# Gate pieces spread over background steps, and high and low part of the activations in one product of 512 columns

## The chip, the core and the metric

The kernel runs on one core of a Trainium2 chip as one program. The metric is the device time of one execution in microseconds (us); three runs of the kernel before have a median of 1888.35 us (1887.22 to 1891.27). The engines are named as the profile names them: PE is TensorE's matmul and PEld its weight load, DVE is VectorE, ACT is ScalarE, POOL is GpSimd and SP is SyncE. An engine works off its own queue in the order written; a DMA is issued by an engine's queue ("ACTq" is an issue on ScalarE's queue).

## What is computed

One decoder block on 256 tokens of width 2048: a gated mixer, and then PEER, a layer that picks 128 of 16384 one-neuron experts per token (8 heads, 16 each). The change touches only PEER:

```python
q = (x @ w_query).reshape(T, 8, 2, 128)               # 16 column tiles of 128
s1, s2 = q[:, :, 0] @ sub_keys_1.T, q[:, :, 1] @ sub_keys_2.T
v1, i1 = top_k(s1, 16); v2, i2 = top_k(s2, 16)        # per half, then of the 16*16 sums
gates = softmax(top_k(v1[:, None] + v2[None, :], 16)) # 8*16 gates per token
act = gelu(x @ expert_down.T)                         # all 16384 experts: 128 tiles of 128
y   = (gates * act) @ expert_up                       # only rows that some token uses
```

The kernel computes the activation of every expert, and turns the gates into a dense array (expert by token), stored beside the activations in a scratch array in HBM, agD. From this it makes a list of the experts used, gathers their rows of agD and of expert_up, and multiplies.

## The kernel before

**Products in two parts.** A float32 matrix is split into a high part H (the value rounded to the format that TensorE takes at one column per cycle) and a low part L, the rest. Activations stand in hF, [128, 16, 2, 256]: for each of 16 slices k of the width, the high part of 256 tokens (index 0) and behind it the low part (index 1). A product is three products: H by high, H by low, L by high; `gemm_k` issues them for one k, 256 columns each, all into the same 256 columns of a PSUM bank:

```python
mm(o, H[:, ks], hT[:, k, 0, :], start=first, stop=False)     # L161
mm(o, H[:, ks], hT[:, k, 1, :], start=False, stop=False)     # L162
mm(o, L[:, ks], hT[:, k, 0, :], start=False, stop=last)      # L163
```

**The tiles.** A tile of weights is 128 by 2048, 1 MB, in one of three buffers raw, loaded by SP. `load_split` (L139) splits it in two halves of 1024: H by ACT (L152), L by DVE (L153). There are three buffers for H and three for L, so a half can be split when TensorE has ended the half three before it. 16 tiles make the queries (names ps_q; the first two are worked side by side), then 128 tiles the activations (ps_z). After a query tile ACT copies the sums to SBUF (`q_copy`, L588), and TensorE multiplies them by the keys (ps_sc, L595). After a down tile ACT applies gelu to the PSUM bank (L1034), and every fourth tile its queue issues the store of four of them to agD (L1036).

**The background.** Beside these products the rest of PEER runs as a list of pieces, bg, each with an estimated cost, in this order: top-k of the 8 heads for token tile 0, softmax, gates of chunk 0; top-k of four heads for tile 1, gates of chunk 1; the other four, softmax; a modulation vector (`adas`, 8 pieces, each a 1 MB load and two DVE passes), chunk 2, the second modulation vector, chunk 3; then the list of experts used (`list_a` to `list_d`). After each tile, `background(step)` takes pieces as long as their summed cost is below BG_RATE times the step. A chunk is 64 tokens: 8 gate units (one-hot products, ps_G, copied to the buffer gch), then 8 pieces `gate_out`, each a store of 16 experts per partition to agD on ACT's queue (L720, 512 KB in runs of 256 B) and a maximum over the chunk on DVE (L722, L725).

The framework sets the order on each engine: it takes the program's dependencies and priorities and writes one queue per engine; H and L have a raised priority. What stands in an engine's queue waits for what stands ahead of it.

**The end.** The last down tile's activations are not stored: they are multiplied by their gates (da, L1054), split (dWH, dWL, L1056 and L1058) and multiplied by the last rows of expert_up (24 products, ps_y, L1065), while the first blocks of the list are gathered (agr, uraw). Then follows a loop over the blocks of the list (L1179), which the change leaves alone.

Of the kernel before, what the change touches and what calls it, by code (L numbers as in the profile page):

```python
# [8 lines left out]
F32 = mybir.dt.float32  # L9
# [4 lines left out]
AF = mybir.ActivationFunctionType  # L14
ALU = mybir.AluOpType
# [25 lines left out]
HP2 = 200  # L41
# [3 lines left out]
def block_kernel(ctx: ExitStack, tc: tile.TileContext, I: dict, out: bass.AP):  # L45
    nc = tc.nc
# [11 lines left out]
    def bank(name):  # L58
        return psp.tile([P, 512], F32, tag="bank", name=name)
# [105 lines left out]
    def gemm_t(src, hT, name, order=tuple(range(KT))):  # L165
        HL = load_split(src)
        ps = bank(name)
        for n, k in enumerate(order):
            gemm_k(ps[:, :T], HL, hT, k, n, n == 0, n == KT - 1)
        return ps  # L170

    def rstd_bcast(ps, tmp_pool, name):
        sd = tmp_pool.tile([P, T], F32, tag="rstd", name=name + "_sd")
# [366 lines left out]
    k = 0  # L540
# [172 lines left out]
    def gate_out(ch, part):  # L713
        tt = ch * TCH // P
        w = P // GP
        sl = slice(part * w, (part + 1) * w)
        g = gch[ch][:, sl, :]
        cs = slice(T + ch * TCH, T + (ch + 1) * TCH)
        e_ = min(sl.stop, NS_E)
        nc.scalar.dma_start(agV[:, sl.start : e_, cs], gch[ch][:, sl.start : e_, :])  # L720
# [6 lines left out]
        if part == GP - 1:  # L727
            nc.scalar.activation(
                gl[:, ch * TCH : (ch + 1) * TCH], gch[ch][:, P - 1 : P, :].rearrange("p a t -> p (a t)"), AF.Copy
            )  # L730
            if ch * TCH % P:
                nc.vector.memset(mk[tt][:, P - 1 : P], 0.0)


# [6 lines left out]
    V = nc.vector  # L741

    def list_a():
        gp_cm[0].__exit__(None, None, None)
        m0, m1, mB, used = lt("la", 4)
        mA, mC, one, tri = lt("lb", 4)
        sA, sB, sC, w = lt("lc", 4)
# [163 lines left out]
    bg = []  # L911

    def topk1(tt, h):
        bg.append((2 * h + 2, 2.4, lambda: topk_a(tt, h)))
        bg.append((2 * h + 2, 4.0, lambda: topk_b(tt, h)))

    def gates(ch):
        n = TCH // 8
        for u in range(n * ch, n * ch + n):
            bg.append((0, 3.1, lambda u=u: gate_unit(u)))  # L920
        for part in range(GP):
            bg.append((0, 9.4 / GP, lambda part=part: gate_out(ch, part)))

    def adas(b):
        for _ in range(8):
            bg.append((0, 2.4, lambda: ada_f[b].piece()))

    def x1_all():
        x1_nat(0)
        x1_nat(1)  # L930
        xp_cm.__exit__(None, None, None)

    bg.append((1, 1.0, x1_all))
    for h in range(8):
        topk1(0, h)
    bg.append((0, 2.0, lambda: softmax(0)))
    gates(0)
    for h in range(4):
        topk1(1, h)
    gates(1)  # L940
    for h in range(4, 8):
        topk1(1, h)
    bg.append((0, 2.0, lambda: softmax(1)))
    adas(0)
    gates(2)
    adas(1)
    gates(3)
    bg.append((0, 8.0, list_a))
    bg.append((0, 5.0, list_b))
    for c in range(16):  # L950
        bg.append((0, 2.5, lambda c=c: list_c(c)))
    bg.append((0, 2.0, list_d))
    bgi = 0
    spent = 0.0

# [9 lines left out]
    for h in range(8):  # L965
        if h == 0:
            pq = [bank("ps_q0"), bank("ps_q1")]
            w2 = [load_raw(I["w_q"][i]) for i in range(2)]
            for half in range(2):
                parts = []  # L970
                for i in range(2):
                    H = wp.tile([P, 1024], F32R, tag="H", bufs=3, name="H")
                    L = wp.tile([P, 1024], F32R, tag="L", bufs=3, name="L")
                    r = w2[i][:, half * 1024 : (half + 1) * 1024]
                    nc.scalar.activation(H, r, AF.Copy)
                    nc.vector.tensor_tensor(L, r, H.bitcast(F32), op=ALU.subtract)
# [23 lines left out]
        )  # L1000

    def open_up():
        ex_cm.__exit__(None, None, None)
        up = R["up"] = ctx.enter_context(tc.tile_pool(name="up", bufs=1, reuse_waits="tile"))
        R["raw"] = [wp.tile([P, 2048], F32, tag="araw", bufs=2, name="uraw") for _ in range(2)]
        R["ag"] = [up.tile([P, 2 * T], F32, name=f"agr{i}") for i in range(NA)]
        R["H"] = [up.tile([P, 2048], F32R, name=f"uH{i}") for i in range(NS)]
        R["L"] = [up.tile([P, 2048], F32R, name=f"uL{i}") for i in range(NS)]
        R["WH"] = [up.tile([P, T], F32R, name=f"uWH{i}") for i in range(NW)]
        R["WL"] = [up.tile([P, T], F32R, name=f"uWL{i}") for i in range(NW)]  # L1010
        R["z"] = up.tile([P, P], BF16, name="zst")
        R["zm"] = up.tile([P, 512], BF16, name="zmv")
        nc.gpsimd.memset(R["z"], 0.0)
        nc.gpsimd.memset(R["zm"], 0.0)
        for b in range(2):
            gather(R["raw"][b], I["up"], idxU, b)
# [10 lines left out]
    actg = None  # L1027
    done_at = NE
    for j in range(NE):
        ps = gemm_t(I["down"][j], hF, "ps_z")  # L1030
        if j % AB == 0:
            actg = ag.tile([P, AB, T], F32, tag="actg", bufs=2, name="actg")
        if j < NE - 1:
            nc.scalar.activation(actg[:, j % AB, :], ps[:, :T], AF.Gelu)  # L1034
        if j % AB == AB - 1 and j < NE - 1:
            nc.scalar.dma_start(agV[:, j - AB + 1 : j + 1, 0:T], actg)  # L1036
        elif j == NE - 2:
            nc.scalar.dma_start(agV[:, j - j % AB : j + 1, 0:T], actg[:, : j % AB + 1, :])
# [10 lines left out]
    nc.scalar.activation(actg[:, (NE - 1) % AB, :], ps[:, :T], AF.Gelu)  # L1049


    dH, dL = load_split(I["up"][NE * P - P : NE * P, :])
    da = up.tile([P, T], F32, name="dact")
    nc.vector.tensor_tensor(da, actg[:, (NE - 1) % AB, :], gl, op=ALU.mult)  # L1054
    dWH = up.tile([P, T], F32R, name="dWH")
    nc.scalar.activation(dWH, da, AF.Copy)  # L1056
    dWL = up.tile([P, T], F32R, name="dWL")
    nc.vector.tensor_tensor(dWL, da, dWH.bitcast(F32), op=ALU.subtract)  # L1058
# [264 lines left out]
```

## Time and profile before

| | |
|---|---|
| median of three runs | 1888.35 us |
| the profiled execution | 1886.62 us, of which its span 1884.8 us |
| mixer, to the first query product | 0 to 509 us |
| queries and down tiles | 509 to 1445 us |
| last down tile's own products and start of the last loop | 1445 to 1461 us |
| loop over the list, end | 1461 to 1885 us |
| PE, DVE, ACT busy | 1796 (95%), 1435 (76%), 875 us (46%) |

The span is the time between the first and the last instruction; the rest of the execution, 1.8 us, lies around it. A busy share is an average over stages; the stage that the change touches is the second.

### The profile page before, as it was taken

How to read it: one execution, taken by the hardware profiler on the slowest of the kernel's cores; microseconds unless marked ns; L12 is line 12 of the kernel's file. 1: busy time of each engine (PE TensorE's matmuls, PEld its weight loads, DVE VectorE, ACT ScalarE, POOL GpSimd, SP SyncE). 2: the span in 40 equal slices, each digit the busy share in tenths (PEclk: the TensorE clock that was granted, in tenths of full speed). 3: DMA queues.
4: the chain of work that ended last, by engine and by line, in shares of the span. 5: the costliest groups of instructions: out<-in, count | busy, mean ns of one | idle time of the engine just before them, and what ended most of it. 6: DMA issues, size and time to landing. Idle time of an engine off the chain costs nothing. (4 is left out here: it accounts for less than half of the span.)

```text
span 1884.8 us, 31863 instructions
## 1 busy us (share of the span) xinstructions
PE 1796.2 (95%) x12820; PEld 1628.0 (86%) x12820; DVE 1434.8 (76%) x2248; ACT 875.1 (46%) x1157; POOL 257.9 (14%) x231
## 2 busy tenths in 40 slices
PE   5889999999999999999999999989998999999995
PEld 3336999999899999999999999989997788888884
DVE  6886889888779877977887777766653777777776
ACT  1116554544554554454345535533343555555654
POOL 0000000000000000000000000000001655656660
PEclk8999999999899999999999999989999999999998
DMA  9996888778565558748787695775565899989992
GB/s 380 352 359 264 342 317 315 272 270 323 189 225 178 190 174 248 225 171 238 230 297 263 196 358 198 218 216 179 179 242 175 321 393 337 324 310 339 320 336 90
DMA packets 153294, 497.21 MB, mean 264 GB/s; under 512 B 75976, under 2 KB 92232, under 8 KB 102064
## 3 DMA queue, kind: packets, MB, share of 16 engines
q1 hardware_dynamic: 47560, 327.55, 47.8%
q0 software_dynamic: 22400, 129.92, 19.0%
q10 hardware_dynamic: 83176, 37.56, 7.3%
q8 instruction: 109, 1.79, 0.4%
q14 instruction: 49, 0.40, 0.1%
HBM read 457.49 MB, written 37.50 MB: 263 GB/s over the span
## 5 line engine op out<-in xcount | busy, mean ns | idle before, releaser
L152 ACT ACTIVATE H<-raw 128x1024 fp32r<-128x1024 f32 x390 | 411.9, 1059 | 575.9 <-PE ps_z L162 386.5
L153 DVE TENSOR_TENSOR L<-raw,H 128x1024 fp32r<-128x1024 f32 x390 | 473.8, 1220 | 227.7 <-ACT H L152 226.0
L161 PE MATMUL ps_z<-hT_f,H 128*128 128x256 f32 x2048 | 586.3, 286 | 7.2 <-ACT H L152 7.2
L163 PE MATMUL ps_z<-hT_f,L 128*128 128x256 f32 x2048 | 581.4, 284 | 5.2 <-DVE L L153 5.2
L162 PE MATMUL ps_z<-hT_f,H 128*128 128x256 f32 x2048 | 581.3, 284 | 0.0
L161 PEld LDWEIGHTS ps_z<-hT_f,H 128*128 128x128 f32 x2048 | 394.5, 193 | 9.5 <-ACT H L152 7.7
L163 PEld LDWEIGHTS ps_z<-hT_f,L 128*128 128x128 f32 x2048 | 394.4, 193 | 6.1 <-DVE L L153 6.1
L162 PEld LDWEIGHTS ps_z<-hT_f,H 128*128 128x128 f32 x2048 | 394.9, 193 | 0.0
L1157 DVE TENSOR_TENSOR uL<-uraw,uH 128x1024 fp32r<-128x1024 f32 x194 | 228.7, 1220 | 101.2 <-ACT uH L1140 98.3
L1140 ACT ACTIVATE uH<-uraw 128x1024 fp32r<-128x1024 f32 x194 | 194.9, 1052 | 176.1 <-PE ps_y L1179 146.1
L113 DVE SCALAR_TENSOR_TENSOR acc<-araw,sT,acc 128x512 f32<-128x512 f32 (+1 forms) x240 | 243.8, 1017 | 7.4 <-DMA araw<-ada_gf 2.0
L1179 PE MATMUL ps_y<-uH,uWH 128*128 128x512 f32 x584 | 229.5, 393 | 2.6 <-issue 2.6
L1179 PE MATMUL ps_y<-uH,uWL 128*128 128x512 f32 x584 | 227.5, 390 | 0.0
L1179 PE MATMUL ps_y<-uL,uWH 128*128 128x512 f32 x584 | 227.4, 389 | 0.0
L998 POOL DMA_INDIRECT agr<-agD,idxG x99 | 138.6, 1400 | 131.0 <-DVE uWL L1159 95.0
L998 POOL DMA_INDIRECT uraw<-up,idxU x99 | 107.8, 1089 | 222.5 <-DVE idxU L882 137.2
L1179 PEld LDWEIGHTS ps_y<-uH,uWH 128*128 128x128 f32 x584 | 110.0, 188 | 24.8 <-issue 3.0
L1179 PEld LDWEIGHTS ps_y<-uH,uWL 128*128 128x128 f32 x584 | 109.6, 188 | 22.8
L1179 PEld LDWEIGHTS ps_y<-uL,uWH 128*128 128x128 f32 x584 | 109.7, 188 | 22.1
L209 PE MATMUL ps_v<-w,xhat 128*128 128x512 f32 x192 | 97.7, 664 | 9.8 <-ACT xhat L180 9.8
L209 PEld LDWEIGHTS ps_v<-w,xhat 128*128 128x128 f32 x192 | 39.3, 212 | 58.9 <-issue 48.4
L161 PE MATMUL ps_q<-hT_f,H 128*128 128x256 f32 x256 | 74.3, 295 | 4.2 <-ACT hT_f L549 3.4
(380 smaller groups left out, 2697.6 us busy)
## 6 DMA issues: line engine op xcount, KB each, us to landing
raw<-down SPq DMA_DIRECT2D x128, 1024.0 KB, 5.0
araw<-ada_sm SPq DMA_DIRECT2D x32, 1024.0 KB, 7.7
raw<-w_ct SPq DMA_DIRECT2D x32, 1024.0 KB, 7.1
araw<-ada_sf SPq DMA_DIRECT2D x32, 1024.0 KB, 6.6
araw<-ada_gm SPq DMA_DIRECT2D x16, 1024.0 KB, 4.8
raw<-w_out SPq DMA_DIRECT2D x16, 1024.0 KB, 4.9
raw<-w_q SPq DMA_DIRECT2D x16, 1024.0 KB, 4.9
araw<-ada_gf SPq DMA_DIRECT2D x16, 1024.0 KB, 6.2
```

The costliest lines, as they stand in the source:

```text
L113: nc.vector.scalar_tensor_tensor(acc, w, sc_, acc, op0=ALU.mult, op1=ALU.add)
L152: nc.scalar.activation(H, r, AF.Copy)
L153: last_l[0] = nc.vector.tensor_tensor(L, r, H.bitcast(F32), op=ALU.subtract).ins
L161: mm(o, H[:, ks], hT[:, k, 0, :], start=first, stop=False)
L162: mm(o, H[:, ks], hT[:, k, 1, :], start=False, stop=False)
L163: mm(o, L[:, ks], hT[:, k, 0, :], start=False, stop=last)
L209: mm(bk, h, w[:, off + c * 512 : off + (c + 1) * 512], start=first, stop=last)
L998: return nc.gpsimd.indirect_dma_start(out_, None, tab, bass.IndirectOffsetOnAxis(ap=idx[:, b : b + 1], axis=0))
L1140: a.activation(H[:, c], raw[:, c], AF.Copy).then_inc(s_h, 1)
L1157: v.tensor_tensor(L[:, c], raw[:, c], H[:, c].bitcast(F32), op=ALU.subtract).then_inc(s_l, 1)
L1179: m_ = t.matmul(ps_y[tt][c], x, y[:, cs], start=False, stop=False, skip_group_check=True)
```

## The change

The diff, cut to its core:

```diff
-BG_RATE = 2.56
+BG_RATE = 2.48
+    def gemm_w(o, HL, hT, k, first, last):
+        H, L = HL[0][k // 8], HL[1][k // 8]
+        ks = slice((k % 8) * P, (k % 8 + 1) * P)
+        mm(o, H[:, ks], hT[:, k, :, :].rearrange("p a t -> p (a t)"), start=first, stop=last, ...)
+        mm(o[:, :T], L[:, ks], hT[:, k, 0, :], start=False, stop=last, skip_group_check=True)
+    def join(dst, ps):
+        nc.scalar.activation(dst, ps[:, T:], AF.Copy)
+        nc.vector.tensor_tensor(dst, ps[:, :T], dst, op=ALU.add)
 def q_copy(ps):
-        nc.scalar.activation(qs, ps[:, :T], AF.Copy)
+        join(qs, ps)
-    def gate_out(ch, part): ...
+    def gate_store(ch, part): ...      # the store alone
+    def gate_mask(ch, part, n): ...    # the maximum alone, in n pieces
+    def leave(ch):
+        return [(0, 1.2, lambda p=p: (gate_store(ch, p), gate_mask(ch, p, GP))) for p in range(GP)]
+    bg += [(0, 2.0, lambda: softmax(0))] + units(0)
+    bg += mixed(sum((topk1(1, h) for h in range(4)), []), leave(0))
+    bg += units(1)
+    bg += mixed(sum((topk1(1, h) for h in range(4, 8)), []) + [(0, 2.0, lambda: softmax(1))], leave(1))
+    bg += units(2)
+    bg += mixed(adas(0) + adas(1), leave(2))
+    bg += units(3)
+    bg += [(0, 4.5, lambda p=p: gate_mask(3, p, 2)) for p in range(2)]
+    bg += [(0, 8.0, list_a)]
+    bg += mixed([(0, 5.0, list_b)] + [... list_c ...], [(0, 0.0, lambda p=p: gate_store(3, p)) for p in range(GP)])
 for j in range(NE):
-        ps = gemm_t(I["down"][j], hF, "ps_z")
-            nc.scalar.activation(actg[:, j % AB, :], ps[:, :T], AF.Gelu)
+        ps = gemm_2(I["down"][j], hF, "ps_z")
+        join(z, ps)
+        nc.scalar.activation(z, z, AF.Gelu)
...
+    with tc.high_priority(offset=HP2):   # around da, dWH and dWL
-    nc.vector.memset(big[:, 0:1], 0.0)
```

For each k, the high part of the weights now meets both parts of the activations in one product of 512 columns, whose two halves are two sums in one bank; the low part adds its 256 columns to the first. So the result of a tile is the sum of two halves of the bank: ACT copies the second to SBUF, DVE adds the first (`join`), and only then follows gelu. `mixed` deals the pieces of a chunk's leaving out among the pieces of the work that follows. The stores of chunk 3 go among the pieces of the list, and its maximum is taken in two pieces of 64 experts instead of eight of 16. The last down tiles are stored one by one, not in threes or fours, and da, dWH and dWL get a higher priority: on DVE dWL now stands ahead of the multiplication of the gathered block agr, which stood ahead of it before.

The order on the engines shows what this does at three places. On ACT, the stores of chunk 0 stand as follows before (agD<-gch is a gate store, agD<-actg a store of activations):

```order
L720 DMA agD<-gch 128x16x64
L152 ACTIVATE H<-raw 128x1024 x2
L1034 ACTIVATE actg<-ps_z 128x256
L720 DMA agD<-gch 128x16x64 x2
L152 ACTIVATE H<-raw 128x1024 x2
L1034 ACTIVATE actg<-ps_z 128x256
L720 DMA agD<-gch 128x15x64
L1036 DMA agD<-actg 128x4x256
L728 ACTIVATE gl<-gch 128x64
L152 ACTIVATE H<-raw 128x1024 x2
```

and now:

```order
L734 DMA agD<-gch 128x16x64
L1059 ACTIVATE actg<-actg 128x256
L152 ACTIVATE H<-raw 128x1024 x2
L187 ACTIVATE actg<-ps_z 128x256
L734 DMA agD<-gch 128x16x64
L1059 ACTIVATE actg<-actg 128x256
L152 ACTIVATE H<-raw 128x1024 x2
L187 ACTIVATE actg<-ps_z 128x256
L734 DMA agD<-gch 128x15x64
L152 ACTIVATE H<-raw 128x1024 x2
```

Between the first and the last store of the chunk stood 11 halves H, with two or three stores in one gap at the end; now there are 15, and no gap holds two gate stores. In each of the other chunks there are 15 as well, where there were 9, 11 and 7.

On PE, at the first gate unit after the softmax of tile 0 (ps_gt are the transposes of indices and gates, ps_G the unit's products), before:

```order
L163 MATMUL ps_z<-hT_f,L 128x256
L655 MATMUL ps_gt<-ident,i1s_4419 128x128
L656 MATMUL ps_gt<-ident,i2s_4421 128x128
L657 MATMUL ps_gt<-ident,gate 128x128
L161 MATMUL ps_z<-hT_f,H 128x256
L162 MATMUL ps_z<-hT_f,H 128x256
```

and now:

```order
L177 MATMUL ps_z<-hT_f,L 128x256
L673 MATMUL ps_gt<-ident,i1s_4419 128x128
L674 MATMUL ps_gt<-ident,i2s_4421 128x128
L675 MATMUL ps_gt<-ident,gate 128x128
L722 LDWEIGHTS oh_5928
L722 MATMUL ps_G<-oa_5930,oh_5928 128x128
```

Before, a whole tile (48 products) stood between the transposes and the unit's first product; now the product stands right behind them. Its operands oh and oa are made by DVE from the transposes, and in DVE's queue one L and one join stand between.

On PE, at the scores of the first head (k_4411 and k_4413 are the two keys, qs the queries), before:

```order
L163 MATMUL ps_q_4431<-hT_f,L 128x256
L595 MATMUL ps_sc<-k_4411,qs 128x128
L161 MATMUL ps_q<-hT_f,H 128x256
L162 MATMUL ps_q<-hT_f,H 128x256
L163 MATMUL ps_q<-hT_f,L 128x256
```

and now:

```order
L177 MATMUL ps_q_4431<-hT_f,L 128x256
L613 MATMUL ps_sc<-k_4411,qs 128x128
L176 MATMUL ps_q<-hT_f,H 128x512
L613 MATMUL ps_sc<-k_4413,qs 128x128
L613 MATMUL ps_sc<-k_4411,qs 128x128
```

The scores stand at the same place, directly behind the last query product, but qs is now written by DVE's addition, which stands in DVE's queue behind the L of a half whose H waits for that same product's end.

## Rows read from the trace of the kernel before

**Rows 1.** Busy time by stretch: us, PE, PEld, DVE, ACT, POOL (instructions), PEclk, DMA, GB/s

```profile
527.00:620.00 93.00, 92.00 (x763) 90.78 (x763) 81.31 (x241) 42.77 (x59) 0.00 (x0) 1.00 0.59 206
...
910.00:1000.00 90.00, 90.00 (x753) 90.00 (x752) 80.68 (x160) 40.55 (x51) 0.25 (x1) 1.00 0.77 276
...
1225.00:1250.00 25.00, 18.54 (x131) 18.16 (x130) 16.50 (x56) 6.14 (x9) 0.66 (x2) 0.80 0.84 238
```

**Rows 2.** PE in order of time, down tiles: start, us, line, tiles [idle before]

```profile
1099.79 0.28 PE L161 MATMUL ps_z<-hT_f,H 128*128 128x256 f32 x1
...
1103.27 0.28 PE L163 MATMUL ps_z<-hT_f,L 128*128 128x256 f32 x1
```

**Rows 3.** PE in order of time, last loop, products of 512 columns

```profile
1699.98 0.39 PE L1179 MATMUL ps_y<-uH,uWL 128*128 128x512 f32 x1
...
1705.65 0.39 PE L1179 MATMUL ps_y<-uH,uWH 128*128 128x512 f32 x1
```

**Rows 4.** What PE waited for: us in total, times, longest

```profile
PE ps_z L161 <- ACT H L152: 7.2, 3, 3.5
PE ps_z L163 <- DVE L L153: 5.2, 4, 3.0
...
PE ps_y L1065 <- DVE dWL L1058: 4.1, 1, 4.1
```

**Rows 5.** ACT's queue in order of time, at the stores of chunks 1, 2, 3

```profile
894.48 5.93 ACTq L720 DMA_DIRECT2D agD<-gch  x1
...
1094.84 8.83 ACTq L720 DMA_DIRECT2D agD<-gch  x2
...
1229.15 8.24 ACTq L720 DMA_DIRECT2D agD<-gch  x3
```

**Rows 6.** PE in order of time, behind the stores of chunks 1 and 3

```profile
901.64 0.39 PE L161 MATMUL ps_z<-hT_f,H 128*128 128x256 f32 x1 [2.40 <-ACT H L152]
...
903.48 0.41 PE L161 MATMUL ps_z<-hT_f,H 128*128 128x256 f32 x1
...
906.68 0.38 PE L161 MATMUL ps_z<-hT_f,H 128*128 128x256 f32 x1
...
1242.84 0.41 PE L161 MATMUL ps_z<-hT_f,H 128*128 128x256 f32 x1
...
1247.96 0.40 PE L161 MATMUL ps_z<-hT_f,H 128*128 128x256 f32 x1
```

**Rows 7.** DVE and ACT by line: shapes, count, busy us, mean ns, idle before

```profile
L153 DVE TENSOR_TENSOR L<-raw,H 128x1024 fp32r<-128x1024 f32 x390 | 473.8, 1220 | 227.7 <-ACT H L152 226.0
...
L1159 DVE TENSOR_TENSOR uWL<-agr,uWH 128x256 fp32r<-128x256 f32 x97 | 40.4, 417 | 0.0
...
L725 DVE TENSOR_REDUCE mkp<-gch 128x16 f32<-128x1024 f32 x16 | 18.9, 1211 | 1.9 <-ACT gch L709 1.9
...
L588 ACT ACTIVATE qs<-ps_q 128x256 f32<-128x256 f32 x16 | 5.9, 367 | 0.0
```

**Rows 8.** PE and DVE in order of time, from the transposes to oa

```profile
656.10 0.27 PE L657 MATMUL ps_gt<-ident,gate 128*128 128x128 f32 x1
...
656.41 0.43 DVE L659 CAST it<-ps_gt 128x256 bf16<-128x256 f32 x1 [1.01 <-PE ps_gt L657]
...
659.92 0.68 DVE L690 TENSOR_TENSOR oa<-oh,g 128x1024 bf16<-128x1024 bf16 x1
```

**Rows 9.** PE in order of time, first head's scores

```profile
528.42 0.49 PE L595 MATMUL ps_sc<-k,qs 128*128 128x128 f32 x2 [0.94 <-ACT qs L588]
```

**Rows 10.** PE and DVE in order of time, end of the down tiles

```profile
1444.82 0.28 PE L163 MATMUL ps_z<-hT_f,L 128*128 128x256 f32 x1
...
1461.50 0.49 PE L1179 MATMUL ps_y<-uH,uWH 128*128 128x512 f32 x1 [2.58 <-issue]
...
1450.74 0.43 DVE L1074 TENSOR_TENSOR agr<-agr 128x256 f32<-128x256 f32 x1 [4.76 <-DMA agr<-agD,idxG]
```

**Rows 11.** Busy time by stretch, columns as in rows 1, stores beside modulation loads

```profile
1100.00:1106.00 6.00, 4.05 (x32) 3.64 (x30) 1.12 (x1) 2.21 (x3) 0.00 (x0) 1.00 1.06 404
```

More of the change, by code (lines that the diff above doesn't have):

```diff
@@ L170, in gemm_t, with gemm_2 @@
         return ps
+    def gemm_w(o, HL, hT, k, first, last):
+        H, L = HL[0][k // 8], HL[1][k // 8]
+        ks = slice((k % 8) * P, (k % 8 + 1) * P)
+        mm(o, H[:, ks], hT[:, k, :, :].rearrange("p a t -> p (a t)"), start=first, stop=last, skip_group_check=True)
+        mm(o[:, :T], L[:, ks], hT[:, k, 0, :], start=False, stop=last, skip_group_check=True)
+    def gemm_2(src, hT, name):
+        HL = load_split(src)
+        ps = bank(name)
+        for k in range(KT):
+            gemm_w(ps, HL, hT, k, k == 0, k == KT - 1)
+        return ps
+    def join(dst, ps):
+        nc.scalar.activation(dst, ps[:, T:], AF.Copy)
+        nc.vector.tensor_tensor(dst, ps[:, :T], dst, op=ALU.add)
     def rstd_bcast(ps, tmp_pool, name):
@@ L711, in gate_unit, with gate_store, gate_mask @@
             )
-    def gate_out(ch, part):
+    def gate_store(ch, part):
+        w = P // GP
+        a, e = part * w, min(part * w + w, NS_E)
+        nc.scalar.dma_start(agV[:, a:e, T + ch * TCH : T + (ch + 1) * TCH], gch[ch][:, a:e, :])
+        if part == GP - 1:
+            nc.scalar.activation(
+                gl[:, ch * TCH : (ch + 1) * TCH], gch[ch][:, P - 1 : P, :].rearrange("p a t -> p (a t)"), AF.Copy
+            )
+    def gate_mask(ch, part, n):
         tt = ch * TCH // P
-        w = P // GP
-        sl = slice(part * w, (part + 1) * w)
+        w = P // n
+        sl = slice(part * w, part * w + w)
         g = gch[ch][:, sl, :]
-        cs = slice(T + ch * TCH, T + (ch + 1) * TCH)
-        e_ = min(sl.stop, NS_E)
-        nc.scalar.dma_start(agV[:, sl.start : e_, cs], gch[ch][:, sl.start : e_, :])
         if ch * TCH % P == 0:
@@ L726, in gate_out @@
             nc.vector.tensor_tensor(mk[tt][:, sl], mk[tt][:, sl], m, op=ALU.max)
[L727 to L731, printed above, removed]
+            if part == n - 1:
                 nc.vector.memset(mk[tt][:, P - 1 : P], 0.0)
@@ L913, in topk1, with units, mixed @@
     def topk1(tt, h):
-        bg.append((2 * h + 2, 2.4, lambda: topk_a(tt, h)))
-        bg.append((2 * h + 2, 4.0, lambda: topk_b(tt, h)))
-    def gates(ch):
+        return [(2 * h + 2, 2.4, lambda: topk_a(tt, h)), (2 * h + 2, 4.0, lambda: topk_b(tt, h))]
+    def units(ch):
         n = TCH // 8
[L919 to L922, printed above, removed]
+        return [(0, 3.1, lambda u=u: gate_unit(u)) for u in range(n * ch, n * ch + n)]
+    def leave(ch):
+        return [(0, 1.2, lambda p=p: (gate_store(ch, p), gate_mask(ch, p, GP))) for p in range(GP)]
     def adas(b):
-        for _ in range(8):
-            bg.append((0, 2.4, lambda: ada_f[b].piece()))
+        return [(0, 2.4, lambda: ada_f[b].piece()) for _ in range(8)]
+    def mixed(work, pieces):
+        o, n = [], 0
+        for i, w in enumerate(work):
+            o.append(w)
+            while n < len(pieces) and n < (i + 1) * len(pieces) // len(work):
+                o.append(pieces[n])
+                n += 1
+        return o + pieces[n:]
     def x1_all():
@@ L931, in x1_all @@
         xp_cm.__exit__(None, None, None)
-    bg.append((1, 1.0, x1_all))
+    bg = [(1, 1.0, x1_all)]
     for h in range(8):
[L935 to L952, printed above, removed]
+        bg += topk1(0, h)
+    bg += [(0, 2.0, lambda: softmax(0))] + units(0)
[7 more added lines that the diff above has]
+    bg += [(0, 8.0, list_a)]
+    bg += mixed(
+        [(0, 5.0, list_b)] + [(0, 2.5, lambda c=c: list_c(c)) for c in range(16)],
+        [(0, 0.0, lambda p=p: gate_store(3, p)) for p in range(GP)],
+    )
+    bg += [(0, 2.0, list_d)]
     bgi = 0
@@ L1002, in open_up @@
     def open_up():
+        gp_cm[0].__exit__(None, None, None)
         ex_cm.__exit__(None, None, None)
@@ L1029, in block_kernel @@
     for j in range(NE):
[L1030 removed]
+        ps = gemm_2(I["down"][j], hF, "ps_z")
         if j % AB == 0:
             actg = ag.tile([P, AB, T], F32, tag="actg", bufs=2, name="actg")
[L1033 to L1035 removed]
+        z = actg[:, j % AB, :]
+        join(z, ps)
+        nc.scalar.activation(z, z, AF.Gelu)
+        if j < NE - AB and j % AB == AB - 1:
             nc.scalar.dma_start(agV[:, j - AB + 1 : j + 1, 0:T], actg)
[L1037 to L1038 removed]
+        elif NE - AB <= j < NE - 1:
+            nc.scalar.dma_start(agV[:, j : j + 1, 0:T], actg[:, j % AB : j % AB + 1, :])
         background(step)
@@ L1048, in block_kernel @@
     up = R["up"]
-    nc.scalar.activation(actg[:, (NE - 1) % AB, :], ps[:, :T], AF.Gelu)
     dH, dL = load_split(I["up"][NE * P - P : NE * P, :])
     da = up.tile([P, T], F32, name="dact")
-    nc.vector.tensor_tensor(da, actg[:, (NE - 1) % AB, :], gl, op=ALU.mult)
     dWH = up.tile([P, T], F32R, name="dWH")
-    nc.scalar.activation(dWH, da, AF.Copy)
     dWL = up.tile([P, T], F32R, name="dWL")
-    nc.vector.tensor_tensor(dWL, da, dWH.bitcast(F32), op=ALU.subtract)
+    with tc.high_priority(offset=HP2):
+        nc.vector.tensor_tensor(da, actg[:, (NE - 1) % AB, :], gl, op=ALU.mult)
+        nc.scalar.activation(dWH, da, AF.Copy)
+        nc.vector.tensor_tensor(dWL, da, dWH.bitcast(F32), op=ALU.subtract)
     ps_y = [[bank(f"ps_y{tt}{c}") for c in range(4)] for tt in range(2)]
```

5 lines of the change are left out of this document (2 added, 3 removed).

## The prediction

> **What bounds the kernel now.** I read the busy time by stretch first, then TensorE in order of time, then what it waited for. In the query and down stage TensorE is the bound: it is busy 92 of 93 us and 90 of 90 [rows 1]; the reader is to see that every other engine has room there, DVE the least (81 of 93, 81 of 90). A busy TensorE may still be slow, so I take its rate from start to start. 29 products of 256 columns lie between the two starts of [rows 2]: 3.48 us, 0.120 us each, where 256 columns at 2.4 GHz are 0.107. 25 products of 512 lie between those of [rows 3]: 5.67 us, 0.227 each, where 512 columns are 0.213. One line fits both: the columns at 2.4 GHz, and 13 ns for each product with its weight load. Then the waits [rows 4]: in the down stage TensorE waited seven times, 12.4 us, for H or L. ACT's queue tells why: it sat 5.93, 8.83 and 8.24 us issuing gate stores [rows 5], and an H stood behind them.
>
> **The single product.** For each k, three products (3 x 0.120 = 0.360 us) become one of 512 and one of 256 (0.227 + 0.120 = 0.347). That is 0.0132 us, in 144 tiles of 16, 2304 times: 30 us, all on the path. No row shows the two widths in turn. If a column cost what it costs in the narrow products, nothing is saved; if what it costs in the wide ones, 3 x 0.2268 / 2 = 0.340, it is 45 us. I take 30, since both rows lie on the line. A tile then lasts 16 x 0.347 = 5.55 us instead of 5.76.
>
> The Trainium skill, page "TensorE: Matmul & The Clock Gate", section "Back-to-back issue gap", speaks against this: an isolated product's gap is its columns at 2.4 GHz and 2.5 ns. By it 256 columns take 0.109 us, the pair saves 2.5 ns and the whole 6 us. The trace differs, 13 ns at either width; mixed widths no run here shows.
>
> **The stores.** The 12.4 us of waits have a second price: after two of them a product of 256 took 3.20/15 and 5.12/24, 0.213 us, which is 256 columns at 1.2 GHz, until the clock rose again [rows 6]; the mean granted clock of the second stretch was 0.80 of full [rows 1]. 39 products at 0.093 more are 3.6 us. Together 16 us, which go if no store holds ACT up. They are not all gone: a chunk's eight stores and two stores of activations still stand within 15 halves, 42 us, and chunk 2 now leaves while modulation vectors are loaded. There 7.5 down tiles, 6 or 7 vector pieces of 1 MB and 5 MB of stores are near 20 MB in 42 us, 475 GB/s; the highest row beside such stores has 404 at a DMA share of 1.06 [rows 11]. At 400 it is 8 us too slow, of which the loaded buffers cover a part. I charge 5.5 us, between 0 and 13 (the 8 us and one block on ACT again).
>
> The skill agrees on the cause: "DMA: Bandwidth & Descriptors", section "Issuing engines are not separate DMA queues", has all issues share the same 16 DMA engines. By it alone a store on ACT's queue and a load on SP's compete in chunk 2 wherever they are issued.
>
> **The join.** Per tile ACT copies 256 columns, 0.37 us by the copy of a query, and DVE adds, 0.42 by an operation of that shape [rows 7]; gelu stays. ACT is busy 40.6 of 90 us [rows 1]: hidden. DVE is not so free. In the 90 us it worked 80.7, for each 5.76 us 5.16: two L's of 1.22 [rows 7] and 2.72 of background. The background now comes at 2.48/2.56, 2.63. With 2.44 and 0.42 this is 5.49 in a tile of 5.55 us. So it is hidden by 1%, with three half buffers to even it out; short overloads will show. In the queries it has scores beside it, which make the period longer, but the same margin. I charge 3 us there and in the top-k, between 0 and 8. The maximum of chunk 3 comes in two operations of some 4 x 1.21 us [rows 7], each ahead of an L: 1 us, 0 to 3.
>
> **Two new waits on PE.** (a) At the first gate unit the product stands right behind the transposes. From the last transpose at 656.10 DVE needed until 659.92 + 0.68 = 660.60 for the first oa, with one L between [rows 8]; TensorE had a tile to work on meanwhile. Now it waits these 4.5 us, the join between (0.4) and then for the second and third oa (0.8): 5.5 us, and behind a wait of this length some 20 products at the low clock, 2 us. I take 7.5, between 0 (if DVE is far ahead) and 9. Queued behind it on PE are only the tile's own products; ACT and DVE gain time to fill their buffers. (b) The first scores waited 0.94 us for ACT's copy [rows 9]. Now an H (I take 1.1 for four times the columns of the copy), an L of 1.22 and two additions come first: 3.2 us, 2 more, and 1 for the clock: 3, between 1 and 5.
>
> **The end of the down tiles.** From the last product at 1444.82 to the loop's first at 1461.50 are 16.7 us [rows 10], for 24 products that take 5.4 at 0.227. TensorE waited 4.1 of them for dWL [rows 4], since DVE had the gathered block agr ahead of it, which landed at 1450.74 [rows 10]. That wait goes; the join adds 0.8. I take -3.5, between -6 (the clock stays up) and +1 (the loop's entry needs agr anyway, and the last store is issued later).
>
> **At no cost.** The modulation loads on SP are asked for a little less often than once a tile, as before, and POOL's few loads move with them; the buffers of the chunks are given back later, which nothing waits for until the background has ended; the memset that goes took its place behind the last product, not ahead of it; the last activations' stores go out singly behind products that are still running. If one of these covers were gone it would be a store's landing, some us once, inside the bounds of the last term.
>
> **The sum**, against the profiled execution of 1886.6 us: -30 - 16 - 3.5 + 5.5 + 3 + 1 + 7.5 + 3 = -29.5, to 1857. That execution lies 1.7 us under the median of the runs, so I forecast 1858 us.
>
> **Rivals.**
> 1. *The join puts DVE on the path (slower).* Gelu waits in ACT's queue for DVE's addition, the addition waits in DVE's queue behind background, and the next H waits behind gelu: a ring through two queues. If the addition's 0.42 us comes on top of each tile instead of beside it, at some 131 tiles with background (14 of the queries, 117 down tiles) it is 55 us: 1913. It decides from 0.26 us a tile, 34 us in all. For it: the margin of 1%. Against it: three halves of buffer, and an addition that stands behind the L of a half two tiles on. Chance 7%.
> 2. *The narrow products' price is by the column.* Then the single product saves nothing: 1858 + 30 = 1888. For it: only that the mixture is not shown. Against it: the two widths. The skill's 2.5 ns, named above, would be 1882. Chance 8%.
> 3. *The stores hold ACT up as before*, because ten transfers in 42 us are still more than the queue drains. The 16 us stay, less the 4 of my charge that they hold already: 1870. Chance 13%.
> 4. *The covers hold*: neither the first unit nor the scores, DVE nor chunk 2 cost anything, 19 us less: 1839. It needs DVE ahead of TensorE at the transposes, against [rows 8]. Chance 10%.
>
> My forecast keeps 62%.
>
> **Range and chances.** The forecast's own range, from its unknowns taken half together, is 1845 to 1871. To hold 8 in 10 it goes to rival 4 below and past rival 3 above: 1841 to 1877. What can be told from no change is 0.2%, 3.8 us, so 1884.6 to 1892.1. Faster: the forecast, rivals 3 and 4, and a part of 2: 88%. Same: most of 2, 6%. Slower: nearly all of rival 1, 6%.
>
> **What the changed profile would show.** Right: the products' starts 0.227 and 0.120 us apart in turn, a down tile every 5.55 us; no issue of a gate store over some 3 us on ACT but in chunk 2; one wait of 4 to 6 us at the first ps_G, named for oa, and one of 2 to 3 at the first ps_sc, named for qs; dWL ahead of agr, and the loop starting some 13 us after the last down product. Wrong: a start-to-start of 0.240 after the wide product (rival 2); many waits of PE for L, with ACT waiting for DVE's addition before gelu (rival 1); H late behind stores of several us in chunks 0, 1 and 3 (rival 3).

## The result and the profile after

The changed kernel took 1869.64 us in the median of four runs (1867.82 to 1870.24), the kernel before 1888.77 beside it; the ratio is 0.9887, with a 95% interval of 0.9869 to 0.9905. That is 19 us gained where 30 were forecast. The profiled execution has a span of 1867.5 us against 1884.8, 17.3 less, and the sums below are made on that.

First the rate of TensorE. The fence shows TensorE in order of time in a down tile without a wait: start, duration, line, tiles.

```profile
1400.08 0.28 PE L177 MATMUL ps_z<-hT_f,L 128*128 128x256 f32 x1
1400.20 0.40 PE L176 MATMUL ps_z<-hT_f,H 128*128 128x512 f32 x1
1400.44 0.28 PE L177 MATMUL ps_z<-hT_f,L 128*128 128x256 f32 x1
...
1404.32 0.28 PE L177 MATMUL ps_z<-hT_f,L 128*128 128x256 f32 x1
```

The wide and the narrow product start in turn, as they should. But twelve pairs lie between the first and the last row: 4.24 us, 0.3533 for a pair. By the widths alone [rows 2, 3] it was to be 0.347. The narrow product takes its 0.12, the wide one some 0.236 where it has 0.227 among its like. A tile lasts 5.65 us instead of 5.55.

That rate is not the only one. Here are two starts of the wide product, again twelve pairs apart, early in the down tiles:

```profile
654.86 0.39 PE L176 MATMUL ps_z<-hT_f,H 128*128 128x512 f32 x1
...
659.02 0.39 PE L176 MATMUL ps_z<-hT_f,H 128*128 128x512 f32 x1
```

They are 4.16 us apart, 0.3467 a pair, just the price by the widths. In 52 down tiles of the changed kernel TensorE had nothing else to do and no gap between two starts above 0.3 us. Seven of them took 5.55 or 5.56 us and 45 took 5.64 to 5.66, with none in between, and tiles of one kind stand in rows. So the same products in the same order have two rates.

Then what TensorE waited for (us in total, times, longest), in the rows that answer to [rows 4, 8, 9, 10]:

```profile
PE ps_sc L613 <- DVE qs L188: 4.4, 4, 3.4
PE ps_G L722 <- DVE oa L708: 4.3, 1, 4.3
...
PE ps_z L176 <- ACT H L152: 3.0, 2, 2.4
PE ps_y L1089 <- ACT dWH L1081: 2.3, 1, 2.3
PE ps_z L177 <- DVE L L153: 2.0, 3, 0.8
```

H and L cost 5.0 us in five waits, where it was 12.4 in seven. At the gate units one wait of 4.3 us stands where one of 0.9 was, at the scores there are four where there was one of 0.9. The wait for dWL has gone; the one for dWH ahead of it was 1.4 us before. The next fence has their places, in order of time with the idle time before in brackets.

```profile
526.36 0.28 PE L177 MATMUL ps_q<-hT_f,L 128*128 128x256 f32 x1
530.04 0.80 PE L613 MATMUL ps_sc<-k,qs 128*128 128x128 f32 x2 [3.41 <-DVE qs L188]
...
662.36 0.27 PE L675 MATMUL ps_gt<-ident,gate 128*128 128x128 f32 x1
666.95 0.39 PE L722 MATMUL ps_G<-oa,oh 128*128 128x128 bf16 x2 [4.32 <-DVE oa L708]
...
1089.25 0.79 PE L176 MATMUL ps_z<-hT_f,H 128*128 128x512 f32 x1 [2.42 <-ACT H L152]
...
1429.76 0.28 PE L177 MATMUL ps_z<-hT_f,L 128*128 128x256 f32 x1
...
1441.53 0.78 PE L1202 MATMUL ps_y<-uH,uWH 128*128 128x512 f32 x1 [3.35 <-issue]
```

The H that came late at 1089 stood behind stores of chunk 2. ACT's queue in order of time, at chunk 0 and at chunk 2:

```profile
735.10 1.74 ACTq L734 DMA_DIRECT2D agD<-gch  x1
736.93 2.15 ACTq L1061 DMA_DIRECT2D agD<-actg  x1
...
1046.90 7.35 ACTq L734 DMA_DIRECT2D agD<-gch  x1
1054.55 5.61 ACTq L734 DMA_DIRECT2D agD<-gch  x1
...
1078.54 9.48 ACTq L734 DMA_DIRECT2D agD<-gch  x1
```

Chunks 0, 1 and 3 have no issue over 2.4 us; chunk 2 has six of 3.6 to 9.5, counting the activations' stores among its own. By stretch (columns as in [rows 1]; the third is chunk 2, the fourth chunk 3):

```profile
530.00:622.00 92.00, 90.83 (x537) 79.65 (x538) 80.36 (x249) 40.12 (x55) 0.00 (x0) 0.98 0.57 205
915.00:1005.00 90.00, 90.00 (x575) 78.21 (x574) 81.01 (x174) 50.63 (x72) 0.25 (x1) 1.00 0.65 216
1050.00:1096.00 46.00, 40.94 (x210) 33.92 (x209) 34.04 (x34) 17.99 (x29) 0.00 (x0) 0.93 1.02 348
1250.00:1275.00 25.00, 25.00 (x147) 21.94 (x146) 20.80 (x69) 11.38 (x16) 0.00 (x0) 1.00 1.03 293
```

TensorE loses 5 of 46 us in chunk 2 and none in chunk 3, where it had lost 6.5 of 25 [rows 1]. At chunk 2 the DMA engines carry 348 GB/s with a share of 1.02.

The 17.3 us by stage, from the first product of each to the first of the next: the queries took 113.8 us (111.0 before), the down tiles 810.2 (826.2), the end of the down tiles 9.2 (15.0), the last loop 404.2 (401.4); the rest is a start and a tail that differ by 1.1 together.

### The profile page after: what moved, and what is told of

Read it like the earlier page. It is cut to its first block, busy times and chain, and to the rows that moved or that the text cites. A ratio compares the mean times of both kernels' runs of the same rounds, so it can differ in the third digit from the quotient of the medians.

```text
span 1867.5 us, 27509 instructions
## 1 busy us (share of the span) xinstructions
PE 1780.6 (95%) x10516; PEld 1501.2 (80%) x10516; DVE 1476.7 (79%) x2379; ACT 914.3 (49%) x1285; POOL 258.3 (14%) x231
## 5 line engine op out<-in xcount | busy, mean ns | idle before, releaser
L176 PE MATMUL ps_z<-hT_f,H 128*128 128x512 f32 x2048 | 733.8, 402 | 3.0 <-ACT H L152 3.0
L176 PEld LDWEIGHTS ps_z<-hT_f,H 128*128 128x128 f32 x2048 | 386.9, 189 | 97.6 <-ACT H L152 4.0
L177 PEld LDWEIGHTS ps_z<-hT_f,L 128*128 128x128 f32 x2048 | 389.2, 190 | 3.6 <-DVE L L153 3.5
L176 PE MATMUL ps_q<-hT_f,H 128*128 128x512 f32 x256 | 94.7, 410 | 6.9 <-DVE hT_f L576 6.9
L1059 ACT ACTIVATE actg<-actg 128x256 f32<-128x256 f32 x128 | 53.0, 415 | 57.6 <-DVE actg L188 57.6
L162 PE MATMUL ps_wo<-yT,H 128*128 128x256 f32 x256 | 73.8, 288 | 1.8 <-DVE yT L530 1.8
```

Source lines behind the costliest of these rows:

```text
L176: mm(o, H[:, ks], hT[:, k, :, :].rearrange("p a t -> p (a t)"), start=first, stop=last, skip_group_check=True)
L177: mm(o[:, :T], L[:, ks], hT[:, k, 0, :], start=False, stop=last, skip_group_check=True)
L1059: nc.scalar.activation(z, z, AF.Gelu)
```

## The experiments

The kernel before took 1889.72, 1889.79 and 1889.25 us in the three series that follow, so kernels are compared by their ratio to it, or by the stages of their traces. One thing shifts the totals without any edit: the mixer, which is the same in all kernels, reached the first query product at 508.4 us in the profiled executions of the changed kernel and of e11, at 509.3 in the kernel before, and at 511.1 to 512.8 in those of e1 to e3 and e5 to e10. A difference of up to 4 us between two totals can come from there.

**The two halves of the change, each alone.** In the first the kernel before gets `gemm_w`, `join` and the rate; in the second the changed kernel loses them.

```diff
 e1, on the kernel before
-BG_RATE = 2.56
+BG_RATE = 2.48
-        ps = gemm_t(I["down"][j], hF, "ps_z")
+        ps = gemm_2(I["down"][j], hF, "ps_z")      # queries alike; join, then gelu
 e2, on the changed kernel
-BG_RATE = 2.48
+BG_RATE = 2.56
-        ps = gemm_2(I["down"][j], hF, "ps_z")
+        ps = gemm_t(I["down"][j], hF, "ps_z")      # queries alike; gelu from the bank
```

> Kernel before, with the wide and narrow product, the join and the background's rate of 2.48, and the old order of the background. Theory A (the pair costs 0.353 us in turn where the sum had 0.347, and saves half of the 30 us): a tile every 5.65 us, 15 us less, 2 to 5 of them lost to the join at the scores, the blocks of the stores stay: 1875 to 1880. Rival B (the pair saves the 30 us and the spread order loses the rest): 1859 to 1865.

> Changed kernel with the three narrow products, no join and the rate of 2.56: the spread order alone. Theory A: of some 19 us of waits and low clock in the down stage all go, 9 come back at chunk 2 and 7 at the first gate unit, 2 less at the end: 1882 to 1887. Rival B (the spread order loses what the product gains): 1890 to 1900.

They took 1883.75 us (ratio 0.9957, 0.9944 to 0.9971) and 1883.71 (0.9963, 0.9947 to 0.9979). e2 is where theory A had it. In e1 rival B is out, and theory A was 4 us too hopeful. 6 and 6 make 12, and both together have 19; from the first query product on, the profiled executions have 4.4 and 6.6 against 16.3. The traces show where: the four blocks of the stores cost TensorE 20.8 us in e1 (7.0, 4.4, 7.6, 1.8) against 18.8 in the kernel before (1.0, 5.2, 2.6, 10.0), and it waited five times for oa, 6.9 us, where the changed kernel does so once, for 4.3. So the spread order was worth more beside the wide product than alone. That the shorter tile makes what was late later would explain it, but is not shown: 20.8 against 18.8 is less than the loss at one chunk varies between executions (e5 below).

The two halves also say which of them brought the two waits. From the waits of TensorE, e1 first:

```profile
PE ps_G L722 <- DVE oa L708: 6.9, 5, 4.3
PE ps_sc L613 <- DVE qs L188: 4.4, 4, 3.4
```

and e2:

```profile
PE ps_y L1088 <- DVE dWL L1081: 4.2, 1, 4.2
...
PE ps_G L722 <- DVE oa L708: 1.0, 1, 1.0
PE ps_sc L613 <- ACT qs L606: 0.9, 1, 0.9
```

The long wait at the first unit belongs to the product, the join and the rate together, not to the spread order: in e2 48 products of a down tile stand on TensorE between the transposes and the first ps_G, in e1 none, as in the changed kernel. And the wait for dWL stays in e2, which has the new priority at the end, and is gone in e1, which has not. The priority alone didn't buy it.

**Eight wide products, then eight narrow ones.**

```diff
-        for k in range(KT):
-            gemm_w(ps, HL, hT, k, k == 0, k == KT - 1)
+        for k0 in range(0, KT, 8):
+            for k in range(k0, k0 + 8):
+                gemm_H(ps, HL, hT, k, k == 0)
+            for k in range(k0, k0 + 8):
+                gemm_L(ps, HL, hT, k, k == KT - 1)
```

> Changed kernel, the products of a half weight in another order: its eight wide ones, then its eight narrow ones; nothing else. Theory A (the 7 ns of a pair are paid where a narrow product follows a wide one, once per turn of width): 14 of 16 turns per tile go, a tile every 5.56 us, 13 us less: 1855 to 1858. Rival C (the wide product with both parts of the activations takes 236 ns whatever follows): 1868 to 1871. Rival D (a tile shorter by 0.1 us puts DVE on the path, the gain is lost in waits for L): 1862 to 1869 with many waits for L.

1864.86 us, ratio 0.9858 (0.9841 to 0.9876): 5 us less, between theory A and rival C. TensorE in order of time, one tile:

```profile
1396.37 2.00 PE L181 MATMUL ps_z<-hT_f,H 128*128 128x512 f32 x8
...
1401.96 0.40 PE L181 MATMUL ps_z<-hT_f,H 128*128 128x512 f32 x1
```

A tile takes 5.59 us (5.65 before, 5.55 by the widths), 0.06 less in each of 128 down tiles: 8 us, of which the down stage shows 6.6. DVE isn't the cause of what is missing (rival D): no down tile waits for L. So the order of the products matters, which rules out rival C, but with 14 of 16 turns only 0.06 of the 0.10 us go. And there is one rate now: of 55 undisturbed down tiles 54 took 5.59 us.

**Orders and widths by themselves.** Two kernels, each executed once and read for its trace alone, in which five down tiles near the end have products of their own.

```diff
 e4: tile 121 the narrow product into the other half of the bank, 122 to 124 groups of 2, 4, 8, 125 both wide
+        g = (1, 1, 2, 4, 8, 1, 1)[arm]
 e12: columns of the first and the second product of a pair, tiles 121 to 125
+    NWIDE = (512, 512, 512, 384, 256, 512)
+    NNARROW = (256, 128, 384, 384, 128, 256)
```

> Changed kernel, in which down tiles 121 to 125 have orders of their own; a look at start-to-start times of a pair. Tile 121: narrow product into the other half of the bank. 122, 123, 124: groups of 2, 4 and 8 wide, then as many narrow. 125: the low part with both parts of the activations too, 512 columns both (it adds the product of the two low parts). Theory A (a turn of width costs 7 ns): 0.353, 0.350, 0.3485, 0.348, and 0.454 for the two wide ones. Rival E (the narrow product waits for the half bank that the wide one has just written): 0.347 in tile 121, and 0.353 in the groups too. Rival C (the wide product's own 236): 0.353 everywhere, 0.472 in tile 125.

> Changed kernel, in which down tiles 121 to 125 leave out columns of some products (their values are then wrong there): pairs of 512 and 128 columns, 512 and 384, 384 and 384, 256 and 128; in tile 125 512 and 256 with the high part's weights in both. By columns at 2.4 GHz and 13 ns each: 0.293, 0.400, 0.347, 0.187 and 0.347 us a pair. Theory A (unlike widths in turn cost 7 ns more): 0.300, 0.407, 0.347, 0.193, 0.353. Rival J (the price is that of loading the low part's weights behind a wide product): 0.347 in tile 125 and more than 0.347 in the tile of 384 and 384. Rival K (a short product waits for the next weights to be loaded): the pairs with 128 columns lie 30 ns and more above the sum.

TensorE in order of time in e4, the first product of the tiles 121, 122, 123, 124, 125 and 126:

```profile
1392.48 0.40 PE L181 MATMUL ps_z<-hT_f,H 128*128 128x512 f32 x1
...
1398.13 0.64 PE L181 MATMUL ps_z<-hT_f,H 128*128 128x512 f32 x2
...
1403.72 1.09 PE L181 MATMUL ps_z<-hT_f,H 128*128 128x512 f32 x4
...
1409.47 2.02 PE L181 MATMUL ps_z<-hT_f,H 128*128 128x512 f32 x8
...
1415.06 0.40 PE L181 MATMUL ps_z<-hT_f,H 128*128 128x512 f32 x1
...
1422.35 0.39 PE L181 MATMUL ps_z<-hT_f,H 128*128 128x512 f32 x1
```

Over 16 pairs: 5.65 us with the other half of the bank (0.353 a pair, so rival E is out), 5.59 in groups of two, 5.59 in groups of eight, and 7.29 with two wide products, 0.228 each (rival C is out). The tile in groups of four took 5.75, of which 0.13 lie in its third group alone (1.54 us where the others take 1.40). Groups of two already have all that groups of eight have. So the price is not one sum per turn of width, as theory A had it. These are single tiles; for eight and eight, e3 has the same 5.59 in 54.

In e12, the starts of two wide products with n pairs between them, n being 11, 12, 5, 13 and 15:

```profile
1391.30 0.44 PE L185 MATMUL ps_z<-hT_f,H 128*128 128x512 f32 x1
...
1395.04 0.44 PE L185 MATMUL ps_z<-hT_f,H 128*128 128x512 f32 x1
...
1396.66 0.40 PE L185 MATMUL ps_z<-hT_f,H 128*128 128x512 f32 x1
...
1401.62 0.40 PE L185 MATMUL ps_z<-hT_f,H 128*128 128x512 f32 x1
...
1406.12 0.33 PE L185 MATMUL ps_z<-hT_f,H 128*128 128x384 f32 x1
...
1407.86 0.33 PE L185 MATMUL ps_z<-hT_f,H 128*128 128x384 f32 x1
...
1409.07 0.34 PE L185 MATMUL ps_z<-hT_f,H 128*128 128x256 f32 x1
...
1412.08 0.33 PE L185 MATMUL ps_z<-hT_f,H 128*128 128x256 f32 x1
...
1412.72 0.40 PE L185 MATMUL ps_z<-hT_f,H 128*128 128x512 f32 x1
...
1418.02 0.40 PE L185 MATMUL ps_z<-hT_f,H 128*128 128x512 f32 x1
```

| columns of a pair | us a pair | columns and 13 ns each | over it |
|---|---|---|---|
| 384, 384 | 0.348 | 0.347 | 0.001 |
| 512, 256 | 0.353 | 0.347 | 0.006 |
| 512, 256, one set of weights' values | 0.353 | 0.347 | 0.006 |
| 512, 384 | 0.413 | 0.400 | 0.013 |
| 512, 128 | 0.340 | 0.293 | 0.047 |
| 256, 128 | 0.232 | 0.187 | 0.045 |

Like widths cost the sum; 512 columns with 256 or 384 cost 6 and 13 ns more in these tiles, and the pairs with 128 columns 45 and 47. Which weights are loaded makes no difference (rival J is out). With 128 columns a product adds 0.112 or 0.113 us to its neighbour's 0.120 or 0.227 where its columns are 0.053; that is the figure that rival K expected. It is a price of the short product, not of unlike widths. In the mixer of the changed kernel eight float32 products of a single column, each with its own weights, also start 0.112 us apart:

```profile
44.85 1.05 PE L129 MATMUL ps_ada<-ones,acc 128*128 128x1 f32 x8
```

What makes the 6 and the 13 stays open. The 6 is no fixed price of the pair, whatever its cause: in the changed kernel the same pairs ran without it in 7 of 52 tiles, in e1 in 17 of 51. In e1 the tiles go from 5.65 to 5.55 us at the stop of TensorE at 1130 us and stay at 5.65 behind the one at 770, so a stop can change the rate and need not. Whether the 13 comes and goes too, one tile can't show.

**The stores of chunk 2.**

```diff
 e5: POOL issues them
-        nc.scalar.dma_start(agV[:, a:e, ...], gch[ch][:, a:e, :])
+        (nc.gpsimd if ch == 2 else nc.scalar).dma_start(agV[:, a:e, ...], gch[ch][:, a:e, :])
 e6: the vectors go to the gate units of chunks 1 and 2
-    bg += units(1)
+    bg += mixed(units(1), adas(0))
-    bg += units(2)
-    bg += mixed(adas(0) + adas(1), leave(2))
+    bg += mixed(units(2), adas(1))
+    bg += [(0, 1.9, f) for _, _, f in leave(2)]
```

> Changed kernel, the eight stores of chunk 2 issued by POOL instead of ACT; the loads beside them unchanged. Theory F (what TensorE lost at 1055 to 1100, some 9.7 us, comes from ACT blocked in issuing): the waits for H there go: 1860 to 1863. Rival G (the 16 DMA engines are full there, whoever issues): the waits stay, behind loads that land late: 1866 to 1871. Rival H (POOL takes long to issue, the chunk's buffer comes back late and the first units of chunk 3 wait): 1871 to 1885.

> Changed kernel, the pieces of the two modulation vectors mixed with the gate units of chunks 1 and 2, the stores of chunk 2 alone, still issued by ACT. Theory G (stores and loads of vectors together are more than the DMA engines carry): no issue over 3 us in chunk 2, 8 to 10 us less, 1860 to 1862. Rival F (eight stores in 11 halves of weight block ACT by themselves): blocks of 4 to 9 us stay, 1868 to 1873.

e5 took 1869.23 us in the median, ratio 0.9866 (0.9824 to 0.9907), its four runs from 1860.91 to 1869.46; e6 took 1862.91, ratio 0.9841 (0.9802 to 0.9880). In the profile of e5 ACT is no longer held up, and TensorE still loses 6 us there. In order of time, POOL, DVE and TensorE:

```profile
1038.41 9.45 POOL L734 DMA_DIRECT2D agD<-gch  x8 [5.84 <-ACT gl L736]
...
1064.57 2.60 DVE L113 SCALAR_TENSOR_TENSOR acc<-araw,sT,acc 128x1024 f32<-128x1024 f32 x2 [3.64 <-DMA araw<-ada_gf]
...
1068.36 0.58 PE L177 MATMUL ps_z<-hT_f,L 128*128 128x256 f32 x1 [3.49 <-DVE L L153]
```

DVE waited 3.64 us for a piece of the vector that landed late, an L stood behind it in DVE's queue, and TensorE waited 3.49 us for that L. So the loss would be one of capacity, paid by whoever meets it first: ACT in issuing, or DVE in waiting for a load. The 6 us by themselves prove no gain over 9.7: e3, e7, e8 and e9, which leave these stores and loads alone, lose between 5.5 and 9.5 us there. (POOL gave the eight stores out in 10 us, closer than ACT did, so the two kernels differ in that too.) The Trainium skill, page "DMA: Bandwidth & Descriptors", section "Issuing engines are not separate DMA queues", states that transfers run on the same 16 DMA engines whichever engine issues them. The trace agrees: with the stores issued by POOL the vector's load still came 3.64 us late for DVE.

e6 leaves the same eight stores with ACT, in 43 us as before (44), and takes only the vectors away. By stretch, at its chunk 2:

```profile
1122.00:1176.00 54.00, 54.00 (x318) 45.45 (x316) 41.79 (x48) 25.24 (x38) 0.00 (x0) 1.00 0.94 266
```

TensorE loses nothing, which none of the kernels with the vectors beside the stores came to, and the down tiles take 800.0 us instead of 810.2. One issue of 4.19 us is left, behind the store 2.8 us ahead of it, and the buffers cover it. Rival F is out, and theory G, a sum of stores and vectors beyond what the engines carry, is left: 6.7 us by the medians.

**Work between the transposes and the first unit.**

```diff
-    bg += [(0, 2.0, lambda: softmax(0))] + units(0)
-    bg += mixed(sum((topk1(1, h) for h in range(4)), []), leave(0))
+    bg += [(0, 2.0, lambda: softmax(0))] + topk1(1, 0) + units(0)
+    bg += mixed(sum((topk1(1, h) for h in range(1, 4)), []), leave(0))
```

> Changed kernel, the first top-k of the second 128 tokens put between the softmax and the first gate unit, so that two down tiles stand between the transposes and the first ps_G on TensorE (none before; a tile and a half in the kernel before the change). Theory: the first unit's 6.0 us go, the rest stays: 1863 to 1865. Rival (DVE is behind there anyway; the wait comes for the next unit or for L): 1868 to 1871.

1862.12 us, ratio 0.9840 (0.9805 to 0.9875). Three down tiles (96 products) now stand between the transposes and the first ps_G, where two were expected; in the kernel before it was one (48 products), not one and a half. TensorE has no wait at all for oa in its trace, and the down tiles take 799.6 us instead of 810.2. 6 of these are the first unit; at chunk 2 it also lost 5.5 instead of 9.7, which the edit wasn't made for and which lies in the spread named under e5.

**One more operation behind the addition.**

```diff
         nc.vector.tensor_tensor(dst, ps[:, :T], dst, op=ALU.add)
+        nc.vector.tensor_scalar(dst, dst, 1.0, None, op0=ALU.mult)
```

> Changed kernel with the join's work on DVE doubled (each joined tile is multiplied by one after the addition, an operation of the same shape, 0.3 to 0.42 us). If DVE has 1% of room in a tile, as the prediction worked out (5.49 of 5.55 us), 0.3 to 0.4 us a tile come on the path where background runs: 30 to 55 us more, 1900 to 1925. If the room is that of the trace (4.8 of 5.65 us busy beside background), it is hidden but for the chain at the scores: 1869 to 1875.

1874.28 us, ratio 0.9909 (0.9873 to 0.9945): 4.6 more. The new operation takes 0.29 us, two thirds of an addition. The queries take 2.0 more, where the scores wait for the longer chain, and the end of the down tiles 2.0; the down tiles take 810.2 as without it. So DVE had room for 0.29 us a tile beside the join.

**The scores one product later.**

```diff
                 qq.append(q_copy(gemm_2(I["w_q"][2 * h + i], hF, "ps_q")))
+                if i == 0:
+                    scores(*held)
-        scores(*qq)
+        held = qq
+        if h == 7:
+            scores(*qq)
```

> Changed kernel, the scores of a head issued one query product later, so that a whole product stands on TensorE between a query's last product and its scores. Theory: of the 4.1 us that the first scores cost more than before nearly all go, and the later waits for qs of 0.3 to 0.6 us, five of them: 5 to 6 us less, 1863 to 1865. Rival (the top-k comes later too and DVE is then late for the next L): 1868 to 1872.

1860.87 us, ratio 0.9840 (0.9820 to 0.9861), 9 us less where 5 to 6 were expected. The queries take 105.4 us, 8.4 less than in the changed kernel and 5.6 less than before the change: a head takes 12.0 us from its scores to the next, where both other kernels took 12.7. One wait is left, at the last head, whose scores are not moved:

```profile
PE ps_sc L613 <- DVE qs L188: 2.4, 1, 2.4
```

**Together.** e10 has the edits of e3, e6 and e7, e11 that of e9 too.

> Changed kernel with three edits of the runs before: eight wide then eight narrow products, the vectors beside the gate units, one top-k ahead of the first unit. Theory (three separate prices, 4.8, 6.7 and 7.5 us): 1849 to 1853. Rival (the shorter tile takes up room on DVE and the DMA engines, the gains overlap): 1854 to 1862.

> The same with the scores one query product later. Theory: 4 to 6 us less than those three together, 1844 to 1849. Rival (the top-k is late and holds the background up): no less than those three.

1850.59 us, ratio 0.9785 (0.9767 to 0.9804), and 1843.01, ratio 0.9760 (0.9742 to 0.9778). By the medians the gains add up: 4.8, 6.7 and 7.5 off 1869.6 are 1850.6. By the profiled executions, from the first query product on, they overlap: e3, e6 and e7 have 8.0, 11.6 and 11.8 us less than the changed kernel, and e10 23.3. So the agreement of the medians is in part luck, by the mixer that came out longer in each of these executions than in the changed kernel's. e11 is 3.2 less than e10 there, the rest of its 7.6 lies in the mixer. e11 is better than both kernels: 26.6 us below the changed one, 46 below the one before.

## Why the prediction was right, and where not

The direction was right and the time in the range; the forecast was 11.6 us too low. Most of it is one term.

| term of the sum | put at | measured in the profiled execution |
|---|---|---|
| single product | -30 | -15.4: 2304 pairs of 0.360 - 0.3533 us |
| stores, with chunk 2 | -16 + 5.5 | -9.1: 18.8 lost before, 9.7 at chunk 2 after |
| join | +3 | +1.0: three later waits at scores, none in the tiles |
| chunk 3's maximum | +1 | 0: TensorE busy 25.00 of 25 us |
| first gate unit | +7.5 | +6.0: 4.3 of wait, the rest at the low clock |
| first scores | +3 | +4.1: 2.5 of longer wait, the rest low clock and the stage's start |
| end of the down tiles | -3.5 | -5.8, and +2.8 in the loop |
| sum | -29.5 | -16.4, and 0.9 by an earlier start of the queries: -17.3 |

The first term takes every pair at 0.3533; with one tile in seven at 0.3467 it would be some 2 us more, so the table closes to 2 us and no better.

*The single product.* This step failed, in its size: "I take 30, since both rows lie on the line." The line was drawn through streams of one width [rows 2, 3] and read as the one price of a mixture. The mixture has two: the 0.347 of the line in 7 of 52 undisturbed tiles, 0.353 in the other 45. The lower bound, nothing saved, was in the prediction, and the truth lies in the middle; e4 and e12 show that streams of like width keep to the line (0.228 and 0.174 us). What sets the rate of the mixture stays open. Rival 2 had the same weak spot in sight, but with a price of 13 ns a pair instead of 6.5, that is, 0.240 after a wide product. The rule of 2.5 ns, which the Trainium skill, page "TensorE: Matmul & The Clock Gate", section "Back-to-back issue gap", gives for an isolated product, would have given 6 us saved. The trace differs: the pair is 33 ns over its columns' 0.320.

*The stores.* Right in kind and size: four blocks with 18.8 us of waits and low clock went, chunk 2 took 9.7 back, within its bounds of 0 to 13; how near that came to the 5.5 is partly chance, as other executions lost 5.5 to 9.5 there. The reason was the one given, capacity beside the vectors (e5, e6), but the engines carried 348 GB/s there, less than the 400 read from a stretch of 6 us [rows 11]. Rival 3 gave 1870 us, which is the time measured, and is wrong all the same: chunks 0, 1 and 3 hold ACT up for 2.3 us at most. A time that fits is no proof of its mechanism.

*The join.* Hidden, but not by the 1% that was worked out. That margin took the background of one stretch of the kernel before, 2.72 us of DVE a tile [rows 1], scaled it by the background's rate to 2.63, and held it for every tile. The fence by stretch above has the same place after the change: DVE is busy 81.0 of 90 us, 5.09 in a tile of 5.65, which leaves 2.23 for the background beside the halves L and the join. Between 775 and 880 it is 89.8 of 105 us, 4.83 in a tile, and e8 puts 0.29 us more on each tile without a longer down stage. The rate is what the list charges for its pieces by estimate, not what DVE does.

*The first unit and the first scores.* Both came where they were named, for oa and for qs, one of 4.3 us in 4 to 6, one of 3.4 in 2 to 3. e1 and e2 add that the first unit's wait comes with the wide product's plan, not with the spread of the pieces; e7 and e9 that other products in front take either away, three down tiles the first and one query product the second. The prediction's parts of the first, 4.5, 0.4 and 0.8, make 5.7 and not 5.5, which changes nothing.

*The end.* The loop starts 11.8 us after the last down product (13 forecast, 16.7 before [rows 10]); dWL came ahead of agr, as DVE's rows in order of time show:

```profile
1432.30 0.42 DVE L1082 TENSOR_TENSOR dWL<-dact,dWH 128x256 fp32r<-128x256 f32 x1 [0.48 <-ACT dWH L1081]
...
1436.14 0.43 DVE L1098 TENSOR_TENSOR agr<-agr 128x256 f32<-128x256 f32 x1 [3.42 <-DMA agr<-agD,idxG]
```

But the loop itself then took 2.8 us more, its first products 0.43 apart instead of 0.23, at a granted clock of 0.50 where it had been 1.00 in the first 6 us of the loop before:

```profile
1441.00:1447.00 6.00, 5.47 (x14) 3.99 (x14) 3.12 (x4) 1.44 (x3) 4.78 (x5) 0.50 0.53 152
```

And e2 shows that the priority by itself doesn't move dWL.

## What to carry to other kernels

A price per product that was read from a stream of one width need not be the price in a mixture: measure the mixture first, over many tiles, since it can have two rates. Grouped by width it had one, 5.59 us a tile, between the 5.55 and 5.65 of the two. When loads and stores together fill the DMA engines, moving the issue to another engine moves the wait; moving one of the two transfers to where the other does not run takes it away. After a pipeline gets a step longer, look at each place where TensorE needs its result at once, and put a product of something else in front.

## What the runs showed of the hardware

- Products of 512 and 256 columns in turn, each with its own weights, ran at 0.347 or at 0.353 us a pair, whole tiles at a time; 0.347 is what streams of like width cost. In the one tile of each, 512 and 384 cost 13 ns over it and pairs of 384 nothing. Two and two (one tile) and eight and eight (54 tiles) cost 0.349 a pair.
- Short float32 products with their own weights started 0.112 us apart at one column (the mixer), and a product of 128 columns added the same 0.112 to one of 256 or 512 (e12).
- POOL issued eight stores of 512 KB one behind another in 9.45 us, at a place where ACT had been held up for 3.9 to 9.5 us at four of its eight.
- A DMA share of 1.03 in itself costs TensorE nothing (chunk 3, 293 GB/s, 25.00 of 25 us busy); the same share with the vectors' loads beside it, at 348 GB/s, cost it 9.7 us.
